# Giving out the filling products between the attention steps: the excess carried over, and a factor of 0.94 in branch A

## The chip, the cores and the metric

The kernel runs on one core of a Trainium2 chip. The metric is the device time of one execution in microseconds (us). The kernel before takes 470.46 us, the median of 3 runs (470.32 to 470.59).

## The reference

One layer of a decoder block on x of 512 tokens by 1024 channels, in float32. Two attention branches read the same normalised input and share one input projection:

```
u    = rms_norm(x, norm_pre)
proj = u @ w_in           # q_a, kv_a, g_a, z_a, qkv_b, z_b, merge
o_a  = nsa_attention(q_a, compress(...), kv_a..., gates_a)
y_a  = o_a * silu(z_a)
o_b  = moba_attention(qkv_b)
y_b  = o_b * silu(z_b)
m    = sigmoid(gate_a) * (y_a @ w_a) + sigmoid(gate_b) * (y_b @ w_b)
out  = x + rms_norm(m @ w_o, norm_post)
```

Branch A has 8 query heads of width 64 in two groups with shared keys and values. Each head has three softmaxes, over compressed blocks, over selected blocks and over a window, which are added with sigmoid gates. Branch B has 8 heads with a key and a value of their own and one softmax each. Every softmax is causal with a linear penalty for distance. At 512 tokens the selected blocks, the window and branch B's blocks cover the whole causal triangle.

## The kernel before, in words

All products have the accuracy of float32 by splitting: an operand is kept as a rounded high part and a low remainder, and one product of 128 rows is issued as three matmuls (high with high, low with high, high with low, L171 to L173, or L290 to L292 for branch B's values). A weight arrives by DMA from SyncE's queue as `raw_...`, ScalarE (ACT) writes the high part `ws_...` (L118), and VectorE (DVE) the remainder (L119).

The input projection is cut into **chunks**, each of 256 columns: za0, za1 (the gate path of branch A), vb0, vb1 (values of B), zb0, zb1 (gate path of B), qkb0 to qkb3 (queries and keys of B), ga and gb (the merge gates), and later ab and wo for the output. A chunk has two slots of eight **pieces**; a piece is a `yield 0.65`, its guess at the time, and holds three matmuls of 512 columns, twice over for six of 256 columns in vb. `stream_gen` runs through the chunks in a fixed order, and after each piece it also issues a split of the next slot's weight. When a slot is complete, the next call issues the copies out of its PSUM bank: for zb and za a tanh on ACT and a product on DVE, for qkb two or more copies on each of the two (L206 to L226), for vb eight on ACT (L305) and eight on DVE (L306).

The attention is done in 24 **units** in a software pipeline, the loop at L1047. Units 0 to 15 are branch A (`NA` = 16), even ones with the selected keys, odd ones with the window's, and units 16 to 23 are branch B. Round s of the loop issues, for the engines in this order:

- `qk_part(s, (3, 2))`: scores of query tiles 3 and 2 (L943, L944). For each, DVE adds the penalty and takes the minimum (L947), and ACT takes the exponential (L949).
- first gap: `fill(f3)`, filling pieces.
- `qk_part(s, (1, 0))`, then `norm_part(s)`: the sums' reciprocal and the normalisation of p (L955 to L961, tiles 3 and 2 on DVE, 1 and 0 on POOL). In rounds 2 and 3, the transposes of the compressed probabilities of branch A follow (L886), whose copies are `pc_...` (DVE: L892).
- second gap: `fill(f3)`.
- `pv_part(s - 2)`: the probabilities with the values (L998, L999).
- `t_part(s - 1, bank)`, three banks: transposes of p (L982, ten in a round), copied out by ACT (L983) and DVE (L984).
- third gap: `fill(f3)`.

TensorE (PE) executes this in the order in which it is written (`manual_schedule` for PE alone); ACT, DVE, POOL and the DMA issues are ordered by a scheduler at build time. PSUM has eight banks of 512 columns: three with the tag t (transposes), one o (PV), two s (scores) and two mm (the chunks). They rotate within a tag, so a matmul that begins a bank waits until the bank's former content is copied out.

What `fill` gives out is set by three lines before the change: `f3` is what is left of `total` (14 chunks at 10.4 us), shared over the remaining rounds and the three gaps of each, and

```
    def fill(us):
        while us > 0 and ("gb1" not in state["done"]):
            ...
                c = next(sg)
                us -= c
```

gives pieces until the amount is reached or exceeded. What it gives in excess is not remembered by `fill`, only in the sum `state["spent"]`, from which the next round's f3 comes.

Of the kernel before, what the change touches and what calls it, by code (L numbers as in the profile page):

```python
# [41 lines left out]
def hybrid_block(ctx, tc, x, norm_pre, w_in, pe_k, w1_k, w2_k, pe_v, w1_v, w2_v,  # L42
# [384 lines left out]
    stream = early_chunks + fill_chunks + merge_chunks + end_chunks  # L427
    pos = {c.name: i for i, c in enumerate(stream)}

    state = {"done": set(), "spent": 0.0}  # L430
    order = []
    for c in stream:
        order += [(c, 0), (c, 1)]
# [56 lines left out]
    sg = stream_gen()  # L490

    def fill(us):
        while us > 0 and ("gb1" not in state["done"]):
            try:
                c = next(sg)
                us -= c
                state["spent"] += c
            except StopIteration:
                return
# [344 lines left out]
    def cmp_scores(g):  # L844

        sp = ps("s", f"sc_{g}")
        for p in range(P):
            q = qs[f"a{p}"][:, g * 512:g * 512 + 512]
            w = slice(96 - 32 * p, 224 - 32 * p)
            mm(sp, kcs[:, g, w], q, start=(p == 0), stop=False)  # L850
            mm(sp, kcl[:, g, w], q, start=False, stop=(p == P - 1))
        both = s4.tile([128, 1024], F32, tag="s4", name=f"sc_{g}")
        bias, sc = both[:, 0:512], both[:, 512:1024]
        b = bias.rearrange("p (i h n) -> p i h n", i=4, h=4)
        for p in range(P):
            pool.tensor_scalar(b[:, :, p], distc, SL_A[4 * g + p], None, op0=ALU.mult)
        act.activation(sc, sp, AF.Copy)
        csc[g] = both

    def cmp_probs(g):  # L860

        both = csc[g]
        bias, sc = both[:, 0:512], both[:, 512:1024]
        s3 = sc.rearrange("p (a n) -> p a n", n=32)
        tp = ps("t", f"scT_{g}")
        for i in range(NT):
            pe_eng.transpose(tp[:, i * 128:(i + 1) * 128], sc[:, i * 128:(i + 1) * 128], ident)
        dve.tensor_tensor(sc, tp, bias, op=ALU.add)
        st = small.tile([128, 2, 16], F32, tag="cst", name=f"cst_{g}")
        dve.tensor_reduce(st[:, 0], s3, axis=mybir.AxisListType.X, op=ALU.min)  # L870
        dve.tensor_scalar(st[:, 0], st[:, 0], 1e20, None, op0=ALU.min)
        dve.tensor_tensor(s3, s3, st[:, 0, :, None].to_broadcast([128, 16, 32]), op=ALU.subtract)
        act.activation(sc, sc, AF.Exp, scale=-1.0)
        dve.tensor_reduce(st[:, 1], s3, axis=mybir.AxisListType.X, op=ALU.add)
        dve.tensor_scalar(st[:, 1], st[:, 1], 1e-30, None, op0=ALU.max)
        dve.reciprocal(st[:, 1], st[:, 1])
        dve.tensor_tensor(st[:, 1].rearrange("p (i h) -> p i h", i=4), st[:, 1].rearrange("p (i h) -> p i h", i=4),
                          gates[:, :, 4 * g:4 * g + 4], op=ALU.mult)
        dve.tensor_tensor(s3, s3, st[:, 1, :, None].to_broadcast([128, 16, 32]), op=ALU.mult)
        csc[g] = sc  # L880

    def cmp_transpose(g):
        sc = csc[g]
        tp = ps("t", f"tc_{g}")
        for i in range(NT):
            pe_eng.transpose(tp[:, i * 128:(i + 1) * 128], sc[:, i * 128:(i + 1) * 128], ident)  # L886

        for i in range(2):
            t = att.tile([128, T], F32R, name=f"pc_{g}_{i}")
            mine, other = slice(64 * i, 64 * i + 64), slice(64 - 64 * i, 128 - 64 * i)  # L890
            act.activation(t[mine], tp[mine], AF.Copy)
            dve.tensor_tensor(t[other], tp[mine], f(t[mine]), op=ALU.subtract)  # L892
            pcs[g, i] = t
# [27 lines left out]
    def qk_part(u, tiles):  # L921
        un = units[u]
        if NT - 1 in tiles:
            if u not in pst:
                p_start(u)
            pbig[u] = att.tile([128, 1152], F32, tag="p", bufs=2, name=f"p_{u}")
        bias = bias_of(un["bias"], un["slope"])
        h = un["half"]
        for i in tiles:
            if i == 0 and un["k"] == "kw":  # L930
                continue
            sp = ps("s", f"s_{u}_{i}")
            n = 128 * (i + 1)
            nn = max(n, 256)
            q = qs[un["q"]][:, h * 512 + i * 128:h * 512 + i * 128 + 128]
            if i == 0 and un["k"] == "ks":
                p_start(u + 1)
                hi, lo = kpair[:, h], klos[0][:, :, h, 0:128]
                todo = [(u, sp[:, 0:128]), (u + 1, sp[:, 128:256])]
            else:  # L940
                hi, lo = kst[un["k"]][:, h * 512:h * 512 + nn], klo[un["k"]][:, h, 0:nn]
                todo = [(u, sp[:, 0:n])]
            mm(sp[:, 0:nn], q, hi, start=True, stop=False)  # L943
            mm(sp[:, 0:nn], q, lo, start=False, stop=True)  # L944
            for v, src in todo:
                pp, st = p_of(v, i), pst[v]
                dve.tensor_tensor_reduce(pp, src, bias[:, 384 - 128 * i:512], 1.0, 3.0e38, ALU.add, ALU.min,  # L947
                                         st[:, 0, i:i + 1])
                act.activation(pp, pp, AF.Exp, bias=st[:, 0, i:i + 1], scale=-1.0, accum_out=st[:, 1, i:i + 1])  # L949

    def norm_part(u):
        un = units[u]
        st = pst[u]
        r = st[:, 1]
        dve.tensor_scalar(r, r, 1e-30, None, op0=ALU.max)  # L955
        dve.reciprocal(r, r)
        if un["gate"] is not None:
            dve.tensor_tensor(r, r, gates[:, :, un["gate"]], op=ALU.mult)  # L958
        for i in range(NT - 1, -1, -1):
            pp = p_of(u, i)  # L960
            (dve if i >= 2 else pool).tensor_scalar(pp, pp, st[:, 1, i:i + 1], None, op0=ALU.mult)  # L961
# [26 lines left out]
    def pv_part(u):  # L988
        un = units[u]
        first, last = un["first"], un["last"]  # L990
        if first:
            ostate["o"] = ps("o", f"o_{u}")
        o = ostate["o"]
        vn, vh = un["v"]
        v = vst[vn].rearrange("p (t h w) -> p t h w", t=4, h=2)
        for j in range(NT):
            q0 = TQ0[j]
            mm(o[:, q0 * 128:512], v[:, j, vh], pt_of(u, 0, j), start=(first and j == 0), stop=False)  # L998
            mm(o[:, q0 * 128:512], v[:, j, vh], pt_of(u, 1, j), start=False,  # L999
               stop=(last and j == 3 and un["cmp"] is None))  # L1000
        if last and un["cmp"] is not None:
            g, p = un["cmp"]
            mm(o, vcs[:, p % 2, g], pcs[g, p // 2], start=False, stop=True)
        if last:
            zt, half = un["z"]
            mine, other = slice(64 * half, 64 * half + 64), slice(64 - 64 * half, 128 - 64 * half)
            t = small.tile([128, T], F32, tag="ev", name=f"ot_{u}")
            act.activation(t[mine], o[other], AF.Copy, scale=0.5)
            dve.scalar_tensor_tensor(t[mine], o[mine], 0.5, t[mine], op0=ALU.mult, op1=ALU.add)  # L1009
            pool.tensor_tensor(zs[zt][mine], t[mine], zs[zt][mine], op=ALU.mult)  # L1010
            if half == 1 and zt >= 4:
                split_y(zt - 4)
                split_y(zt)
# [15 lines left out]
    NA = len(units)  # L1029
# [4 lines left out]
    NU = len(units)  # L1034

    state["spent"] = 0.0
    cmp_scores(0)
    fill(1.4)
    cmp_probs(0)

    def need(u):
        if u >= NA and (u - NA) % 2 == 0:
            drain_to(f"qkb{(u - NA) // 2}")

    total = sum(10.4 for c in stream[pos["za0"]:pos["gb1"] + 1])
    with tc.manual_schedule(engines={mybir.EngineType.PE}):
        for s in range(NU + 2):  # L1047
            f3 = max(0.0, total - state["spent"]) / (NU + 2 - s) / 3
            if s < NU:
                need(s)  # L1050
                qk_part(s, (3, 2))
            fill(f3)
            if s < NU:
                qk_part(s, (1, 0))
                norm_part(s)
            if s == 1:
                cmp_scores(1)
            if s in (2, 3):
                cmp_transpose(s - 2)
            if s == 1:  # L1060
                fill(f3 / 2)
                cmp_probs(1)
                fill(f3 / 2)
            else:
                fill(f3)
            if 0 <= s - 2:
                pv_part(s - 2)
            if 0 <= s - 1 < NU:
                for bank in range(3):
                    t_part(s - 1, bank)  # L1070
            fill(f3)
# [82 lines left out]
```

## Time and profile before

| | |
|---|---|
| median of 3 runs | 470.46 us (470.32 to 470.59) |
| profiled execution, its own time | 470.35 us |
| its span on the core | 468.6 us |
| granted TensorE clock, mean | 0.997 |
| PE busy | 458.2 us |
| DVE busy | 326.1 us |
| ACT busy | 253.9 us |
| POOL busy | 125.5 us |

The span is the time from the first to the last instruction on the core; 1.75 us of the execution lie around it. Times in the rows are from the span's start. PE's matmuls are pipelined, so a row's own duration is longer than its distance to the next one; the distance between starts is what a matmul costs in a row of them. In a row, "<-DVE q_b L210" in brackets says that the engine was idle for so long ahead of the instruction, and that DVE's operation of line 210 released it.

### The profile page before, as it was taken

Reading aid. Unit: us, or ns where it says so; the run is one execution under the profiler, and the core shown is the slowest. Engines: PE = TensorE matmul, PEld = TensorE weight load, DVE = VectorE, ACT = ScalarE, POOL = GpSimd, SP = SyncE. Lnnn points to the kernel's source line nnn. Section 1 sums busy time; section 2 is a strip of 40 time slices with the busy share of each in tenths; the row PEclk is TensorE's granted clock in tenths of the full one; section 3 lists DMA queues with packets and bytes.
Section 4 is the critical chain, followed back from the end, with each engine's and each line's share of the span. In section 5 each row is a group of like instructions: output and inputs, shape, how many; then the busy total and the mean of one; then the engine's idle time right before and its main releaser. Section 6 shows DMA issues by size and latency. Waiting matters only on the chain.

```text
span 468.6 us, 6999 instructions
## 1 busy us (share of the span) xinstructions
PE 458.2 (98%) x2408; PEld 389.8 (83%) x2408; DVE 326.1 (70%) x837; ACT 253.9 (54%) x684; POOL 125.5 (27%) x144
## 2 busy tenths in 40 slices
PE   8999999999999999999989999999999999999994
PEld 7888887889999888888878888888888888888884
DVE  3858767898878768878887888696674264275044
ACT  6755656666667566566667667675433333234021
POOL 6500007322432313423133454323221010020000
PEclk9999999999999999999999999999999999999998
DMA  8667125023202203032022023032135324223133
GB/s 281 187 162 199 50 50 171 8 85 91 70 21 91 72 19 90 8 84 92 19 72 90 1 90 80 12 92 80 57 94 143 109 61 134 90 90 136 45 134 136
DMA packets 45091, 42.08 MB, mean 90 GB/s; under 512 B 1624, under 2 KB 39808, under 8 KB 45056
## 3 DMA queue, kind: packets, MB, share of 16 engines
q1 hardware_dynamic: 44912, 41.12, 29.8%
q10 hardware_dynamic: 144, 0.52, 0.3%
q8 instruction: 19, 0.31, 0.3%
q14 instruction: 16, 0.13, 0.1%
HBM read 39.54 MB, written 2.10 MB: 89 GB/s over the span
## 4 chain that ended last, share of the span: by engine, by line
PE 94%; DVE 3%; POOL 1%; ACT 1%; issue 1%; POOLq 0%; DVEq 0%; ACTq 0%
PE t L982 5%; PE o L999 3%; PE o L998 3%; PE mm_gb L171 3%; PE mm_gb L173 3%; PE mm_gb L172 3%; PE s L943 3%; PE mm_qkb L171 3%; PE mm_qkb L172 3%; PE mm_qkb L173 3%; PE s L944 3%; PE mm_ga L171 3%; PE mm_ga L173 3%; PE mm_ga L172 3%; PE pa L626 2%; PE mm_vb L290 2%
## 5 line engine op out<-in xcount | busy, mean ns | idle before, releaser
L949 ACT ACTIVATE p<-p,st 128x512 f32<-128x512 f32 (+3 forms) x96 | 53.2, 555 | 45.1 <-DVE st L947 44.8
L961 POOL TENSOR_SCALAR p<-p,st 128x256 f32<-128x256 f32 (+1 forms) x48 | 43.8, 922 | 72.5 <-DVE st L958 53.3
L984 DVE TENSOR_TENSOR pt<-t,pt 128x512 fp32r<-128x512 f32 (+1 forms) x72 | 39.1, 592 | 1.9 <-ACT pt L983 1.6
L947 DVE CUSTOM_DVE_ANT_0 p<-s,bias_a 128x512 f32<-128x512 f32 (+3 forms) x64 | 29.2, 485 | 12.6 <-PE s L944 12.2
L983 ACT ACTIVATE pt<-t 128x512 fp32r<-128x512 f32 (+1 forms) x72 | 32.8, 528 | 4.8 <-PE t L982 4.2
L354 POOL TENSOR_TENSOR ga<-ga,gb 128x512 f32<-128x512 f32 x8 | 11.7, 1466 | 76.2 <-DVE gb L353 76.2
L982 PE MATMUL t<-ident,p 128*128 128x128 f32 x240 | 30.1, 273 | 0.0
L982 PEld LDWEIGHTS t<-ident,p 128*128 128x128 f32 x240 | 27.0, 140 | 0.8
L1010 POOL TENSOR_TENSOR z<-ot,z 64x512 f32<-64x512 f32 x16 | 20.7, 1295 | 24.4 <-DVE ot L1009 24.4
L171 PE MATMUL mm_qkb<-uh,ws_qkb 128*128 128x512 f32 x64 | 25.9, 405 | 1.3 <-DVE q_b L210 1.3
L119 DVE TENSOR_TENSOR ws_ab<-raw_ab,ws_ab 128x256 fp32r<-128x256 f32 x32 | 12.7, 454 | 20.0 <-ACT ws_ab L118 20.0
L171 PE MATMUL mm_ga<-uh,ws_ga 128*128 128x512 f32 x64 | 25.6, 400 | 0.0
L171 PE MATMUL mm_gb<-uh,ws_gb 128*128 128x512 f32 x64 | 25.6, 400 | 0.0
L961 DVE TENSOR_SCALAR p<-p,st 128x512 f32<-128x512 f32 (+1 forms) x48 | 24.9, 556 | 0.6
L172 PE MATMUL mm_qkb<-ul,ws_qkb 128*128 128x512 f32 x64 | 25.3, 395 | 0.0
L173 PE MATMUL mm_gb<-uh,ws_gb 128*128 128x512 f32 x64 | 25.3, 395 | 0.0
L173 PE MATMUL mm_ga<-uh,ws_ga 128*128 128x512 f32 x64 | 25.3, 395 | 0.0
L172 PE MATMUL mm_gb<-ul,ws_gb 128*128 128x512 f32 x64 | 25.3, 395 | 0.0
L172 PE MATMUL mm_ga<-ul,ws_ga 128*128 128x512 f32 x64 | 25.3, 395 | 0.0
L173 PE MATMUL mm_qkb<-uh,ws_qkb 128*128 128x512 f32 x64 | 25.3, 395 | 0.0
L901 POOL TENSOR_SCALAR bias_a<-dbase 128x512 f32<-128x512 f32 x8 | 13.2, 1650 | 32.1 <-DVE st L947 31.9
L901 POOL TENSOR_SCALAR bias_b<-dbase 128x512 f32<-128x512 f32 x8 | 12.2, 1528 | 35.5 <-DVE st L947 35.5
(312 smaller groups left out, 1386.8 us busy)
## 6 DMA issues: line engine op xcount, KB each, us to landing
raw_qkb<-in_w_in_dram SPq DMA_DIRECT2D x8, 512.0 KB, 5.1
raw_ga<-in_w_in_dram SPq DMA_DIRECT2D x4, 1024.0 KB, 5.1
raw_gb<-in_w_in_dram SPq DMA_DIRECT2D x4, 1024.0 KB, 5.2
raw_wo<-in_w_o_dram SPq DMA_DIRECT2D x4, 1024.0 KB, 5.0
raw_qa<-in_w_in_dram SPq DMA_DIRECT2D x4, 512.0 KB, 6.5
raw_za<-in_w_in_dram SPq DMA_DIRECT2D x4, 512.0 KB, 5.2
raw_vb<-in_w_in_dram SPq DMA_DIRECT2D x2, 1024.0 KB, 5.2
raw_zb<-in_w_in_dram SPq DMA_DIRECT2D x2, 1024.0 KB, 6.0
```

The lines of the kernel that those rows point to most:

```text
L171: mm(dst, v[:, 0, k], rh(n), start=(n == 0), stop=False)
L172: mm(dst, v[:, 0, k], rl(n), start=False, stop=False)
L173: mm(dst, v[:, 1, k], rh(n), start=False, stop=(n == len(kts) - 1))
L901: pool.tensor_scalar(t, dbase, slope, None, op0=ALU.mult)
L943: mm(sp[:, 0:nn], q, hi, start=True, stop=False)
L947: dve.tensor_tensor_reduce(pp, src, bias[:, 384 - 128 * i:512], 1.0, 3.0e38, ALU.add, ALU.min, st[:, 0, i:i + 1])
L949: act.activation(pp, pp, AF.Exp, bias=st[:, 0, i:i + 1], scale=-1.0, accum_out=st[:, 1, i:i + 1])
L961: (dve if i >= 2 else pool).tensor_scalar(pp, pp, st[:, 1, i:i + 1], None, op0=ALU.mult)
L982: pe_eng.transpose(tp[:, b * 128:(b + 1) * 128], p_of(u, i)[:, 128 * j:128 * j + 128], ident)
L983: act.activation(h[:, c0:c0 + n], tp[:, 0:n], AF.Copy)
L984: dve.tensor_tensor(l[:, c0:c0 + n], tp[:, 0:n], f(h[:, c0:c0 + n]), op=ALU.subtract)
L1010: pool.tensor_tensor(zs[zt][mine], t[mine], zs[zt][mine], op=ALU.mult)
```

## The change

The state gets an entry `owed`. `fill` adds its amount to it and gives pieces while it is above zero; each piece is subtracted, so that an excess stays there as a negative amount for the next call. The share f3 takes the owed amount into account and is multiplied by 0.94 in the rounds of branch A (s below 16). The whole diff:

```diff
--- before.py
+++ after.py
@@ -427,7 +427,7 @@
     stream = early_chunks + fill_chunks + merge_chunks + end_chunks
     pos = {c.name: i for i, c in enumerate(stream)}
 
-    state = {"done": set(), "spent": 0.0}
+    state = {"done": set(), "spent": 0.0, "owed": 0.0}
     order = []
     for c in stream:
         order += [(c, 0), (c, 1)]
@@ -490,10 +490,11 @@
     sg = stream_gen()
 
     def fill(us):
-        while us > 0 and ("gb1" not in state["done"]):
+        state["owed"] += us
+        while state["owed"] > 0 and "gb1" not in state["done"]:
             try:
                 c = next(sg)
-                us -= c
+                state["owed"] -= c
                 state["spent"] += c
             except StopIteration:
                 return
@@ -1045,7 +1046,8 @@
     total = sum(10.4 for c in stream[pos["za0"]:pos["gb1"] + 1])
     with tc.manual_schedule(engines={mybir.EngineType.PE}):
         for s in range(NU + 2):
-            f3 = max(0.0, total - state["spent"]) / (NU + 2 - s) / 3
+
+            f3 = max(0.0, total - state["spent"] - state["owed"]) / (NU + 2 - s) / 3 * (0.94 if s < NA else 1.0)
             if s < NU:
                 need(s)
                 qk_part(s, (3, 2))
```

One line is added above L494 and one more above L1049, so that a line of the loop's helpers, such as L947, is L948 in the changed kernel. The same instructions are issued, in another order. Pieces in a round before: nine in rounds 0 to 21 (ten in round 1), six in round 22 and the rest at the end. Now: eight in rounds 0 to 7, 9 to 11, 13 and 15, nine in rounds 8, 12, 14 and 16 to 22, and the rest at the end.

Three places show what this moves. The names: mm_ is a chunk's PSUM bank with the chunk and a running number, t_ and o_ are the banks of transposes and PV, pt0 and pt1 the transposed probabilities, st the softmax sums.

**PE, the first product of chunk zb0.** Before, in round 6:

```order
L999 MATMUL o_4_1742<-pt0_826,v_slc_126 128x256
L998 MATMUL o_4_1742<-pt0_826,v_slc_126 128x256
L999 MATMUL o_4_1742<-pt0_826,v_slc_126 128x256
L982 MATMUL t_5_0_1751<-ident_78,p0_5_1427 128x128
L982 MATMUL t_5_0_1751<-ident_78,p_5_1530 128x128 x3
L982 MATMUL t_5_1_1758<-ident_78,p_5_1530 128x128 x4
L982 MATMUL t_5_2_1765<-ident_78,p_5_1530 128x128 x2
L171 MATMUL mm_zb0_0_1778<-uh_76,ws_zb0_0_1645 128x512
```

Now, in round 7:

```order
L291 MATMUL mm_vb1_1_1578<-ws_vb1_1_1585,uh_76 128x256
L292 MATMUL mm_vb1_1_1578<-ws_vb1_1_1585,ul_77 128x256
L290 MATMUL mm_vb1_1_1578<-ws_vb1_1_1585,uh_76 128x256
L291 MATMUL mm_vb1_1_1578<-ws_vb1_1_1585,uh_76 128x256
L292 MATMUL mm_vb1_1_1578<-ws_vb1_1_1585,ul_77 128x256
L171 MATMUL mm_zb0_0_1801<-uh_76,ws_zb0_0_1709 128x512
L172 MATMUL mm_zb0_0_1801<-ul_77,ws_zb0_0_1709 128x512
L173 MATMUL mm_zb0_0_1801<-uh_76,ws_zb0_0_1709 128x512
L999 MATMUL o_4_1681<-pt1_827,v_win_127 128x512
```

Before, the products of PV and the ten transposes stand ahead of zb0's first product, now the last products of vb1, and PV follows.

**DVE, the copies out of vb1's two banks (mm_vb1_0 and mm_vb1_1).** Before, in round 6, when zb0's first product follows:

```order
L306 TENSOR_TENSOR v_b3_1692<-mm_vb1_0_1522,v_b3_1692 128x2x64
L955 TENSOR_SCALAR st_6_1655<-st_6_1655 128x4
L956 RECIPROCAL st_6_1655<-st_6_1655 128x4
L958 TENSOR_TENSOR st_6_1655<-st_6_1655,gates_103 128x4
L961 TENSOR_SCALAR p_6_1656<-p_6_1656,st_6_1655 128x512
L306 TENSOR_TENSOR v_b3_1692<-mm_vb1_0_1522,v_b3_1692 128x2x64
L961 TENSOR_SCALAR p_6_1656<-p_6_1656,st_6_1655 128x384
L306 TENSOR_TENSOR v_b2_1687<-mm_vb1_1_1523,v_b2_1687 128x2x64
```

Now, in round 7:

```order
L956 TENSOR_SCALAR st_7_1649<-st_7_1649 128x4
L306 TENSOR_TENSOR v_b3_1752<-mm_vb1_0_1577,v_b3_1752 128x2x64
L957 RECIPROCAL st_7_1649<-st_7_1649 128x4
L959 TENSOR_TENSOR st_7_1649<-st_7_1649,gates_103 128x4
L306 TENSOR_TENSOR v_b2_1747<-mm_vb1_1_1578,v_b2_1747 128x2x64
L962 TENSOR_SCALAR p_7_1726<-p_7_1726,st_7_1649 128x512
L306 TENSOR_TENSOR v_b3_1752<-mm_vb1_0_1577,v_b3_1752 128x2x64
L962 TENSOR_SCALAR p_7_1726<-p_7_1726,st_7_1649 128x384
```

Both times the last copy out of mm_vb1_0 stands between the two normalisations; now the first copy out of mm_vb1_1 is ahead of it as well, before it was behind.

**DVE, round 2, the compressed probabilities.** The two operations pc_0_0 and pc_0_1 empty the bank tc_0. Before:

```order
L119 TENSOR_TENSOR ws_vb0_1_1275<-raw_vb0_955,ws_vb0_1_1275 128x256
L892 TENSOR_TENSOR pc_0_0_1189<-tc_0_1184,pc_0_0_1189 64x512
L955 TENSOR_SCALAR st_2_1135<-st_2_1135 128x4
L119 TENSOR_TENSOR ws_vb0_1_1275<-raw_vb0_955,ws_vb0_1_1275 128x256
L956 RECIPROCAL st_2_1135<-st_2_1135 128x4
L119 TENSOR_TENSOR ws_vb0_1_1275<-raw_vb0_955,ws_vb0_1_1275 128x256
L958 TENSOR_TENSOR st_2_1135<-st_2_1135,gates_103 128x4
L892 TENSOR_TENSOR pc_0_1_1192<-tc_0_1184,pc_0_1_1192 64x512
L961 TENSOR_SCALAR p_2_1136<-p_2_1136,st_2_1135 128x512
L961 TENSOR_SCALAR p_2_1136<-p_2_1136,st_2_1135 128x384
```

Now:

```order
L119 TENSOR_TENSOR ws_vb0_0_1223<-raw_vb0_955,ws_vb0_0_1223 128x256
L956 TENSOR_SCALAR st_2_1120<-st_2_1120 128x4
L119 TENSOR_TENSOR ws_vb0_0_1223<-raw_vb0_955,ws_vb0_0_1223 128x256
L957 RECIPROCAL st_2_1120<-st_2_1120 128x4
L893 TENSOR_TENSOR pc_0_0_1172<-tc_0_1167,pc_0_0_1172 64x512
L959 TENSOR_TENSOR st_2_1120<-st_2_1120,gates_103 128x4
L119 TENSOR_TENSOR ws_vb0_0_1223<-raw_vb0_955,ws_vb0_0_1223 128x256
L962 TENSOR_SCALAR p_2_1121<-p_2_1121,st_2_1120 128x512
L962 TENSOR_SCALAR p_2_1121<-p_2_1121,st_2_1120 128x384
L893 TENSOR_TENSOR pc_0_1_1175<-tc_0_1167,pc_0_1_1175 64x512
```

Both normalisations (the last operations on p_2, of 512 and 384 columns) stood behind pc_0_1, and now stand ahead of it.

## Rows read from the trace of the kernel before

**Rows 1.** The page's first part: busy us (share) xinstructions of each engine
```profile
PE 458.2 (98%) x2408; PEld 389.8 (83%) x2408; DVE 326.1 (70%) x837; ACT 253.9 (54%) x684; POOL 125.5 (27%) x144
```

**Rows 2.** Stretches: us, PE, PEld, DVE, ACT, POOL busy (x), PEclk, DMA share, GB/s
```profile
100.70:111.10 10.40, 10.40 (x59) 9.00 (x58) 10.01 (x32) 7.05 (x20) 1.79 (x2) 1.00 0.04 5
200.00:240.00 40.00, 38.71 (x202) 32.59 (x201) 32.20 (x92) 26.53 (x74) 11.77 (x12) 1.00 0.24 71
456.00:469.00 13.00, 6.53 (x52) 6.16 (x51) 5.27 (x13) 2.22 (x8) 1.10 (x2) 0.89 0.39 142
```

**Rows 3.** Timeline, PE, round 15: start, us, engine, line, operation [idle before <-releaser]
```profile
235.61 0.40 PE L173 MATMUL mm_qkb<-uh,ws_qkb 128*128 128x512 f32 x1
237.30 0.47 PE L171 MATMUL mm_qkb<-uh,ws_qkb 128*128 128x512 f32 x1 [1.29 <-DVE q_b L210]
```

**Rows 4.** Timeline, ACT, round 15
```profile
234.53 0.59 ACT L206 ACTIVATE q_b<-mm_qkb 64x512 fp32r<-64x512 f32 x1 [0.30 <-PE s L943]
```

**Rows 5.** Timeline, DVE, round 15
```profile
236.46 0.69 DVE L210 SCALAR_TENSOR_TENSOR q_b<-mm_qkb,q_b 64x512 fp32r<-64x512 f32 x1
```

**Rows 6.** Timeline, PE, round 22
```profile
304.79 0.39 PE L173 MATMUL mm_ga<-uh,ws_ga 128*128 128x512 f32 x1
...
306.14 0.39 PE L171 MATMUL mm_ga<-uh,ws_ga 128*128 128x512 f32 x1
```

**Rows 7.** Timeline, DVE, round 22
```profile
303.30 0.69 DVE L1020 TENSOR_TENSOR ys_b<-z,ys_b 128x512 fp32r<-128x512 f32 x1 [0.83 <-ACT ys_b L1019]
...
304.57 0.68 DVE L947 CUSTOM_DVE_ANT_0 p<-s,bias_b 128x512 f32<-128x512 f32 x1
```

**Rows 8.** Timeline, PE, round 6 from its second gap
```profile
145.08 0.28 PE L290 MATMUL mm_vb<-ws_vb,uh 128*128 128x256 f32 x1
...
147.08 0.28 PE L292 MATMUL mm_vb<-ws_vb,ul 128*128 128x256 f32 x1
...
148.50 1.25 PE L982 MATMUL t<-ident,p 128*128 128x128 f32 x10
149.51 0.47 PE L171 MATMUL mm_zb<-uh,ws_zb 128*128 128x512 f32 x1
```

**Rows 9.** Timeline, DVE, round 6, after its scores
```profile
147.39 0.49 DVE L961 TENSOR_SCALAR p<-p,st 128x512 f32<-128x512 f32 x1
147.79 0.28 DVE L306 TENSOR_TENSOR v_b<-mm_vb,v_b 128x128 fp32r<-128x128 f32 x1
```

**Rows 10.** Timeline, PE, round 2
```profile
103.99 0.60 PE L886 MATMUL tc<-ident,sc 128*128 128x128 f32 x4
...
107.81 1.26 PE L982 MATMUL t<-ident,p 128*128 128x128 f32 x10
```

**Rows 11.** Timeline, DVE, round 2
```profile
103.04 0.68 DVE L879 TENSOR_TENSOR sc<-sc,cst 128x512 f32<-128x512 f32 x1
...
107.55 0.69 DVE L892 TENSOR_TENSOR pc<-tc,pc 64x512 fp32r<-64x512 f32 x1
108.28 1.08 DVE L961 TENSOR_SCALAR p<-p,st 128x512 f32<-128x512 f32 x2
```

**Rows 12.** Timeline, PE, round 0, first gap
```profile
82.43 0.40 PE L171 MATMUL mm_za<-uh,ws_za 128*128 128x512 f32 x1
...
84.54 0.28 PE L943 MATMUL s<-k_ks,q_a 128*128 128x256 f32 x1
```

**Rows 13.** Timeline, DVE, round 0
```profile
83.88 0.55 DVE L947 CUSTOM_DVE_ANT_0 p<-s,bias_a 128x384 f32<-128x384 f32 x1
```

**Rows 14.** Timeline, PE, round 6, scores and first gap
```profile
141.66 0.40 PE L943 MATMUL s<-k_ks,q_a 128*128 128x512 f32 x1
...
142.48 0.28 PE L290 MATMUL mm_vb<-ws_vb,uh 128*128 128x256 f32 x1
```

**Rows 15.** Timeline, DVE, round 6, first tile of the unit
```profile
142.59 0.68 DVE L947 CUSTOM_DVE_ANT_0 p<-s,bias_a 128x512 f32<-128x512 f32 x1
```

**Rows 16.** Timeline, DVE, qkb3's k copies
```profile
238.04 0.68 DVE L223 TENSOR_TENSOR klos<-mm_qkb,k_b 64x512 fp32r<-64x512 f32 x1
```

## The prediction

> **What bounds the kernel now.** I read the busy times first. TensorE (PE) is busy for 458.2 of the 468.6 us of the span, VectorE (DVE) for 326.1, ScalarE (ACT) for 253.9 [rows 1]. The reader should see that this leaves PE 10.4 us without work in all. The table by stretches says where: PE is busy in all of 10.40 us in round 2 of the attention loop, in 38.71 of 40 us between 200 and 240 us, and in only 6.53 of the last 13 us, at a granted clock of 1.00, 1.00 and 0.89 [rows 2]. The change does not touch the last 13 us nor the first products. So the loop is a solid row of matmuls, and a change of order alone can win only the few gaps in it. The start times of neighbouring matmuls show them: 512 columns follow each other in 0.234 us (from 82.43 to 84.54 us, nine of them [rows 12]), 256 columns in 0.118 (seventeen in 2.00 us [rows 8]). Only two places in the loop lie more than 0.4 us above this.
>
> Gap one is in round 15. The first product of chunk qkb3 starts 1.69 us after the matmul ahead of it [rows 3]; less the usual 0.23 that is 1.46 us. It waits for its PSUM bank: ACT copies qkb2's query half out of it only at 234.53 [rows 4], and DVE takes the second half of the remainder at 236.46 for 0.69 us [rows 5]. The matmuls into that bank were done in round 14; the copies stood behind unit 15's exponentials on ACT. Gap two is in round 22: five matmuls (one of 512, four of 256 columns) take 1.35 us from 304.79 to 306.14 [rows 6], where 0.23 + 4 x 0.118 = 0.70 is usual, so 0.65 us is lost. Unit 22's first score tile leaves its bank on DVE at 304.57, behind a split of a branch product at 303.30 that had itself waited for ACT [rows 7].
>
> **The change part by part.** No instruction is added or removed; filling pieces (0.70 us of PE each) move. Before, every call rounds up to whole pieces, so nine stand in nearly every round until they run short in round 22 (six). Now the excess is remembered and the share is cut to 0.94 in branch A: eight in most of rounds 0 to 15 and nine in rounds 16 to 22. After round 15 there are 131 pieces handed out instead of 145, and the 14 missing ones fill rounds 22 to 24. Their weight splits (ACT and DVE) and DMA loads move with them, later in number of rounds; DMA is busy for 0.24 of 200 to 240 us and 0.04 of round 2 [rows 2], so I cost the loads at nothing. If that cover failed, a chunk's first product would wait for a load, and I see no load near its due time.
>
> *Gain, round 15.* qkb2's query half is now finished in round 16's first gap, its copies stand behind two of unit 16's exponentials, and the bank is next wanted in round 17, some 9 us of PE work later. The 1.46 us go. *Gain, round 22.* Its first gap has three pieces instead of two and no branch split ahead of the score: 0.65 us go; at least 0.4, if that bank stays a little late. Together 2.1 us (1.85 to 2.1); I take 2.05.
>
> *New wait, round 7 (second gap).* Chunk zb0 now follows the last product of vb1 directly. In round 6 before, PV and the transposes stood between: vb1's last product started at 147.08, zb0's first at 149.51 [rows 8]. With X the end of the scores (145.08), DVE finished the last copy of vb1's bank 0 at 147.79 + 0.28 = X + 2.99 [rows 9], 1.4 us before it was needed. Now the bank is wanted after two pieces, at X + 12 x 0.118 = X + 1.41, and on DVE the last copy of bank 0 stands behind bank 1's first copy, and, as before, the 512-column normalisation. From below: bank 1's last product ends at X + 1.57, then an ACT copy (taken as 0.28, like its DVE remainder), the remainder (0.28), the normalisation (0.40 from its start to the next) and the last copy (0.28) give X + 2.8, a wait of 1.4 [rows 9]. From above: the old X + 2.99 plus the copy put ahead (0.28) is X + 3.3, a wait of 1.9. I take 1.7, since DVE has little slack.
>
> *New wait, round 2 (transposes).* The third transpose bank is the one that the compressed scores' transposes used. These started at 103.99, and the transposes at 107.81, at 0.1 us each, so the third bank was wanted after eight, at 108.6, which is 4.6 after 103.99 [rows 10]. DVE freed it with its second pass at 107.55 + 0.69 = 108.24, 4.25 after [rows 11]. Only 0.35 us was to spare. Now both normalisations (1.08 us) and a 0.68 us addition that used to run earlier, at 103.04, stand ahead of that pass [rows 11], while a 0.68 us operation on za moves behind it: 4.25 + 1.08 = 5.3 after, a wait of 0.7, and without credit for the za operation, and with the wait for the reciprocal, up to 6.4, a wait of 1.8. I take 1.5, near the upper end, since DVE has 10.01 us of work in a round of 10.40 [rows 2] and does not catch up.
>
> *New wait, round 0.* With two pieces in the first gap instead of three, the last score tile wants its bank after 6 x 0.234 + 2 x 0.118, at 84.07 by the old times [rows 12]. DVE frees it at 83.88 + 0.55 = 84.43 [rows 13]. 0.4 us (0.2 to 0.6).
>
> *New wait, round 6 (first gap).* vb1's second bank is wanted one piece after the scores: 0.82 (from 141.66 to 142.48) + 0.70 = 1.52 us after the scores start [rows 14]. The last copy out of it now stands behind the unit's first tile, which DVE started 0.93 us after the scores, for 0.68 [rows 15]; with 0.28 for the copy it is free at 1.8 to 1.9. 0.3 us (0 to 0.6).
>
> *Rounds 2 (scores) and 19.* A few DVE operations that fell elsewhere now stand ahead of a unit's first tile: four weight splits on ACT in round 2, the k copies of qkb3 in round 19 (0.68 for one of 512 columns [rows 16]). One such operation late at worst, nothing at best: 0.2 each (0 to 0.6).
>
> Sum of the new waits: 0.4 + 0.2 + 1.5 + 0.3 + 1.7 + 0.2 = 4.3 us (2.3 to 6.1). Net: 4.3 - 2.05 = +2.25. The profiled execution took 470.35 us, so 472.6; the median is 0.11 above it, so **472.7 us**. The unknown ends give 470.6 (2.3 with a gain of 2.1) to 474.7 (6.1 with 1.85).
>
> **A rule that speaks against the change.** The row first: after the 1.29 us wait in round 15 the granted clock of 200 to 240 us still reads 1.00 [rows 2, 3]. In a sentence by itself: the Trainium skill, "TensorE: Matmul & The Clock Gate", section "A second HAM failure mode: psum-queue depth-cycling", says that a TensorE which idles briefly between groups while it cycles through PSUM banks swings between its clock levels and loses throughput beyond the idling. By that rule the new bank waits would cost more than their length; by the row they cost their length, and that is what I add.
>
> **The rivals.** *The new waits are hidden* (the other side, faster). The mechanism is the copy out of a bank in time, and round 7 decides: if DVE finishes bank 0 within 1.41 us of the scores, and the third transpose bank comes within 4.6 us of the compressed transposes, 0.5 us of the rest remains: 470.46 - 2.05 + 0.5 = 468.9. Break-even is at 2.05 us of new waits. For it: these engines are ordered by a scheduler, and delays met early give DVE time to catch up later. Against it: DVE's order in both rounds puts the freeing pass behind work that cannot start sooner. *The balance*: the new waits stay near their low ends, 1.2 to 2.9 in sum: 469.6 to 471.4, no change that can be told. *DVE becomes the bound of rounds 1 to 3*: eight pieces make a round 0.70 us shorter, 10.40 - 0.70 = 9.70, under DVE's 10.01 [rows 2], and the lag is paid in each of these rounds: 8 x 0.3 = 2.4 us more if eight rounds are as full, 475.1. For it: the row. Against it: later rounds leave DVE more slack, and splits move out with the pieces. *The clock falls* after a 2 us wait: one round of about 10 us at half rate, 483. Against it: the row of round 15. *The change doesn't do what it says*: the order shows that the pieces move, so I give this nothing.
>
> **How the numbers follow.** A measurement of this kernel can tell 0.2% (0.94 us) from no change. Forecast as it stands, slower, 471.4 to 474.7: 0.50. DVE as the bound: 0.14. Clock: 0.04. Balance, within 0.2%: 0.20. Hidden, faster: 0.12. So slower is 0.68. The range leaves out the clock and the ends of the two neighbours, about 0.2 in all: 469.6 to 475.2; the forecast's own is 471.4 to 474.7.
>
> **What would show it.** Right: no wait of qkb3's first product on DVE in the list of waits, and none over 0.3 us in round 22; instead a stop of 1.4 to 1.9 us ahead of zb0's first product put down to DVE's copies of vb, one of 0.7 to 1.8 inside a set of ten transposes in round 2 put down to the compressed pass, and one near 0.4 in round 0. PE's busy time stays near 458 and the span grows. Wrong: no stop ahead of zb0, or a granted clock under 1.00 inside the loop, or waits spread over many rounds with DVE full.

## The result, and the profile after

The changed kernel takes 473.11 us (median of 4 runs, 472.98 to 473.47), the kernel before 470.39 us (4 runs, 470.32 to 470.59): a ratio of 1.0058, 95% interval 1.0046 to 1.0070. It is slower by 2.7 us. The profiled execution took 473.22 us with a span of 471.4.

The busy times of the changed kernel (us, share of the span, instructions), to compare with [rows 1]:

```profile
PE 460.7 (98%) x2408; PEld 390.8 (83%) x2408; DVE 326.3 (69%) x837; ACT 254.5 (54%) x684; POOL 126.3 (27%) x144
```

The same 2408 matmuls are busy for 2.5 us more. What that means is said at the end; the stops are better read from the starts of matmuls. The list of waits (engine, operation and line <- what released it: us in total, times, longest) has lost the wait of qkb3's first product, and has new ones:

```profile
PE mm_zb L171 <- DVE v_b L306: 1.4, 1, 1.4
...
PE s L944 <- DVE st L948: 0.5, 2, 0.3
...
PE t L983 <- DVE pc L893: 0.5, 1, 0.5
```

In stretches (us, then PE, PEld, DVE, ACT and POOL busy, granted clock, DMA share, GB/s), the gap of [rows 2] between 200 and 240 us is closed. Most of the loop's idle time now lies between 70 and 160 us (the loop starts at 81.7, round 7 ends near 159). The granted clock is 1.00 in both kernels. First the kernel before, then the changed one:

```profile
70.00:160.00 90.00, 89.80 (x561) 80.00 (x560) 75.25 (x229) 59.16 (x174) 33.65 (x39) 1.00 0.24 70
```

```profile
70.00:160.00 90.00, 87.51 (x546) 77.48 (x546) 75.00 (x228) 58.34 (x170) 35.96 (x40) 1.00 0.24 71
200.00:240.00 40.00, 40.00 (x213) 34.29 (x213) 32.48 (x97) 25.49 (x72) 13.79 (x13) 1.00 0.19 53
```

**The largest new stop** is in round 7, ahead of zb0's first product. PE first, then DVE:

```profile
151.27 0.28 PE L945 MATMUL s<-klos,q_a 128*128 128x256 f32 x1
...
152.69 0.28 PE L292 MATMUL mm_vb<-ws_vb,ul 128*128 128x256 f32 x1
154.37 0.47 PE L171 MATMUL mm_zb<-uh,ws_zb 128*128 128x512 f32 x1 [1.40 <-DVE v_b L306]
```

```profile
153.35 0.28 DVE L306 TENSOR_TENSOR v_b<-mm_vb,v_b 128x128 fp32r<-128x128 f32 x1
153.55 0.48 DVE L962 TENSOR_SCALAR p<-p,st 128x512 f32<-128x512 f32 x1
153.94 0.28 DVE L306 TENSOR_TENSOR v_b<-mm_vb,v_b 128x128 fp32r<-128x128 f32 x1
```

PE has done with vb1 at 152.69 and starts zb0 1.68 us later, where 0.12 is usual. DVE makes the last copy of bank 0 at 153.94, behind bank 1's first copy (153.35) and the normalisation of 512 columns (153.55). It ends at 154.22, and zb0 follows 0.15 later. With X the end of the scores, 151.39 (one distance of 0.12 behind the last score matmul at 151.27), the bank was free at X + 2.8.

**Round 2**, inside the ten transposes, PE and DVE:

```profile
105.95 1.04 PE L983 MATMUL t<-ident,p 128*128 128x128 f32 x8
107.48 0.41 PE L983 MATMUL t<-ident,p 128*128 128x128 f32 x2 [0.49 <-DVE pc L893]
```

```profile
104.31 0.68 DVE L893 TENSOR_TENSOR pc<-tc,pc 64x512 fp32r<-64x512 f32 x1
...
105.44 1.17 DVE L962 TENSOR_SCALAR p<-p,st 128x512 f32<-128x512 f32 x2
106.64 0.69 DVE L893 TENSOR_TENSOR pc<-tc,pc 64x512 fp32r<-64x512 f32 x1
107.36 0.69 DVE L237 SCALAR_TENSOR_TENSOR z<-sg,mm_za 128x512 f32<-128x512 f32 x1
```

Eight transposes start in a row, 0.109 us apart. The ninth should start at 105.95 + 8 x 0.109 = 106.82 and starts at 107.48, 0.66 us late, when DVE has ended its second compressed pass (106.64 + 0.69 = 107.33). Both normalisations (105.44) stand ahead of that pass; the operation on za (107.36) now stands behind it.

**Round 0 and round 6.** The last score tile of round 0 (84.68) follows 0.53 us behind its neighbour instead of 0.12. In round 6 the first product into vb1's second bank (140.32) comes 0.42 after the one ahead of it:

```profile
84.15 0.28 PE L945 MATMUL s<-klos,q_a 128*128 128x256 f32 x1
84.68 0.38 PE L944 MATMUL s<-kpair,q_a 128*128 128x256 f32 x1 [0.25 <-DVE st L948]
```

```profile
139.90 0.28 PE L292 MATMUL mm_vb<-ws_vb,ul 128*128 128x256 f32 x1
140.32 0.36 PE L290 MATMUL mm_vb<-ws_vb,uh 128*128 128x256 f32 x1
```

**Round 4**, which the prediction does not name, DVE and PE:

```profile
120.47 0.67 DVE L237 SCALAR_TENSOR_TENSOR z<-sg,mm_za 128x512 f32<-128x512 f32 x1
```

```profile
121.19 0.39 PE L290 MATMUL mm_vb<-ws_vb,uh 128*128 128x256 f32 x1
```

The operation on za1 (120.47 + 0.67 = 121.14) empties the bank that becomes vb0's second. The first product into it starts at 121.19, 0.26 us behind the matmul ahead of it, and the next one follows 0.23 later, where 0.12 is usual both times. Together 0.25 us are lost.

**Round 19**, which I had put at 0.2 us. PE, and DVE just before:

```profile
268.02 0.40 PE L173 MATMUL mm_ga<-uh,ws_ga 128*128 128x512 f32 x1
268.71 0.39 PE L944 MATMUL s<-k_b,q_b 128*128 128x256 f32 x1 [0.29 <-DVE st L948]
...
269.52 0.40 PE L171 MATMUL mm_ga<-uh,ws_ga 128*128 128x512 f32 x1
```

```profile
265.53 0.42 DVE L225 CAST k_b<-k_b 64x512 fp32r<-64x512 f32 x1
...
266.79 0.69 DVE L224 TENSOR_TENSOR klos<-mm_qkb,k_b 64x512 fp32r<-64x512 f32 x1
267.50 0.42 DVE L226 CAST k_b<-k_b 64x512 fp32r<-64x512 f32 x1
267.95 0.69 DVE L948 CUSTOM_DVE_ANT_0 p<-s,bias_b 128x512 f32<-128x512 f32 x1
```

All four operations on qkb3's keys (265.53 to 267.92) stand ahead of unit 19's first tile (267.95). The second of its two score matmuls starts at 265.58, the next matmul at 265.81. From 268.02 to 269.52 PE needs 1.50 us for five matmuls that usually take 0.70: 0.80 us are lost.

**Round 22**, whose gap I had taken for closed, PE and DVE:

```profile
298.66 0.40 PE L173 MATMUL mm_gb<-uh,ws_gb 128*128 128x512 f32 x1
299.04 0.39 PE L944 MATMUL s<-k_b,q_b 128*128 128x256 f32 x1
...
299.86 0.40 PE L171 MATMUL mm_gb<-uh,ws_gb 128*128 128x512 f32 x1
```

```profile
297.36 0.69 DVE L1021 TENSOR_TENSOR ys_b<-z,ys_b 128x512 fp32r<-128x512 f32 x1 [0.82 <-ACT ys_b L1020]
...
298.30 0.68 DVE L948 CUSTOM_DVE_ANT_0 p<-s,bias_b 128x512 f32<-128x512 f32 x1
```

1.20 us for the same five matmuls: 0.50 us are still lost, against 0.65 in [rows 6]. The split of the branch product (297.36) is still ahead of the score tile (298.30), as in [rows 7].

The gap that did close is the one ahead of qkb3: its first product starts at 246.74, 0.24 us behind the matmul ahead of it. DVE's last copy out of its bank now ends at 241.03 + 0.69 = 241.72, 5.0 us earlier:

```profile
241.03 0.69 DVE L210 SCALAR_TENSOR_TENSOR q_b<-mm_qkb,q_b 64x512 fp32r<-64x512 f32 x1
```

```profile
246.74 0.40 PE L171 MATMUL mm_qkb<-uh,ws_qkb 128*128 128x512 f32 x1
```

### The profile page after: what moved, and what is told of

It reads as the page before. It is cut to its first block, busy times and chain, and to the rows that moved or that the text cites. A ratio compares the mean times of both kernels' runs of the same rounds, so it can differ in the third digit from the quotient of the medians.

```text
span 471.4 us, 6998 instructions
## 1 busy us (share of the span) xinstructions
PE 460.7 (98%) x2408; PEld 390.8 (83%) x2408; DVE 326.3 (69%) x837; ACT 254.5 (54%) x684; POOL 126.3 (27%) x144
## 4 chain that ended last, share of the span: by engine, by line
PE 89%; DVE 7%; ACT 2%; issue 1%; POOL 0%; POOLq 0%; DVEq 0%; ACTq 0%
PE t L983 5%; PE mm_gb L171 3%; PE mm_qkb L171 3%; PE mm_gb L172 3%; PE mm_gb L173 3%; PE mm_qkb L172 3%; PE mm_qkb L173 3%; PE o L999 3%; PE o L1000 3%; PE mm_ga L173 3%; PE mm_ga L171 3%; PE mm_ga L172 3%; PE s L944 3%; PE pa L627 3%; PE s L945 3%; PE mm_zb L171 2%
## 5 line engine op out<-in xcount | busy, mean ns | idle before, releaser
L962 POOL TENSOR_SCALAR p<-p,st 128x256 f32<-128x256 f32 (+1 forms) x48 | 45.4, 955 | 62.8 <-DVE st L959 31.4
L948 DVE CUSTOM_DVE_ANT_0 p<-s,bias_a 128x512 f32<-128x512 f32 (+3 forms) x64 | 29.2, 487 | 13.8 <-PE s L945 13.8
```

## The experiments

Each kernel was run five to nine times, in turn with the kernel before. That one took 470.43 us (9 runs, 470.33 to 470.76) beside "Order on DVE alone" and "All named stops", and 470.34 us (18 runs, 470.01 to 470.98) beside the others. "Pieces 3, 2, 3" means the filling pieces in the three gaps of a round. In the kernels with moved pieces, `fill` takes the number of pieces from a table, which is the kernel's own but for the entries named.

**The factor without the carry** needs no run. It changes nothing: in round 0 a gap's share is 145.6 / 78 = 1.87 us, and 0.94 of it 1.75; both round up to three pieces of 0.65, and the later calls round up alike. The built program has the same instructions in the same order on PE, DVE and ACT as the kernel before.

**The carry without the factor.**

```diff
-            f3 = ... / (NU + 2 - s) / 3 * (0.94 if s < NA else 1.0)
+            f3 = ... / (NU + 2 - s) / 3
```

> The change with the carried excess but the factor 0.94 taken out. Theory (single stops of TensorE at banks that are emptied late, which depend on where a chunk's boundary falls): other boundaries, so other stops. None ahead of zb0's first product and none ahead of qkb3's; 0.5 us in round 0 (two pieces in the first gap again); 1.4 to 2.0 us among round 2's transposes, since its second gap has two pieces instead of three and the bank is wanted 0.7 us sooner; 0.5 us in round 22. In sum about 471.1 us (470.4 to 471.8). Rival (DVE is the bound in rounds of eight pieces, so the loss goes with the number of such rounds): it loses about half of what the change loses, 471.7, spread over rounds 0 to 15 with no stop over 0.5 us.

Measured: 473.39 us, ratio 1.0065 (1.0052 to 1.0077). Both were wrong on the time: the theory by 2.3 us. The stops that it named came, 0.53 us in round 0, 1.76 in round 2 and 0.58 in round 22, but also two that it did not name, 1.2 us in round 12 and 0.9 in round 20. Round 2, then round 12, each PE and DVE:

```profile
106.41 1.04 PE L983 MATMUL t<-ident,p 128*128 128x128 f32 x8
109.05 0.41 PE L983 MATMUL t<-ident,p 128*128 128x128 f32 x2 [1.60 <-DVE pc L893]
```

```profile
105.36 1.04 DVE L962 TENSOR_SCALAR p<-p,st 128x512 f32<-128x512 f32 x2
...
107.15 0.69 DVE L237 SCALAR_TENSOR_TENSOR z<-sg,mm_za 128x512 f32<-128x512 f32 x1
...
108.21 0.69 DVE L893 TENSOR_TENSOR pc<-tc,pc 64x512 fp32r<-64x512 f32 x1
```

```profile
191.71 0.39 PE L173 MATMUL mm_zb<-uh,ws_zb 128*128 128x512 f32 x1
193.08 0.38 PE L944 MATMUL s<-k_kw,q_a 128*128 128x256 f32 x1 [0.98 <-DVE st L948]
```

```profile
189.85 0.42 DVE L225 CAST k_b<-k_b 64x512 fp32r<-64x512 f32 x1 [0.37 <-ACT k_b L221]
...
191.87 0.42 DVE L226 CAST k_b<-k_b 64x512 fp32r<-64x512 f32 x1
192.32 0.69 DVE L948 CUSTOM_DVE_ANT_0 p<-s,bias_a 128x512 f32<-128x512 f32 x1
```

In round 2 the normalisations and the operation on za both stand ahead of the second compressed pass (108.21). In round 12 the chunk qkb0 ends just ahead of the scores, and its four key operations stand ahead of unit 12's first tile, the pattern of round 19 in the changed kernel. The rival falls by the trace: the loss is in five single stops of over 0.5 us each, not spread. It falls by the number of rounds too: this kernel has eight pieces in 8 of the 16 rounds of branch A, the changed kernel in 13, and it loses 3.05 us against 2.72. So it is not the factor that costs; with the full share other boundaries meet, and cost as much.

**One piece moved out of the changed kernel's largest stop.** Round 7: pieces 3, 2, 3 instead of 3, 3, 2.

```diff
-    ..., 3, 3, 2, ...
+    ..., 3, 2, 3, ...
```

> The changed kernel with one filling piece, zb0's first, moved from the second to the third gap of round 7, behind PV and the transposes. Theory: the stop of 1.57 us ahead of it is gone and nothing takes its place: 473.1 - 1.6 = 471.5 us (471.3 to 471.9). Rival (DVE is behind in these rounds, the stop is only where it shows): the lag shows up at the next wait for DVE, and 472.5 to 473.1 remain.

Measured: 471.50 us (9 runs, 471.30 to 472.18), as the theory said. zb0's first product now follows the transposes at their usual distance, with no wait named; the other stops of the changed kernel stand as they were:

```profile
154.75 1.25 PE L982 MATMUL t<-ident,p 128*128 128x128 f32 x10
155.75 0.48 PE L171 MATMUL mm_zb<-uh,ws_zb 128*128 128x512 f32 x1
```

**The same stop put into the kernel before.** Round 6: pieces 3, 4, 2 instead of 3, 3, 3.

```diff
-    ..., 3, 3, 3, ...
+    ..., 3, 4, 2, ...
```

> The kernel before with one filling piece, zb0's first, moved from the third to the second gap of round 6, directly behind vb1's last product. Theory: DVE frees the bank 2.99 us after the scores, and it is now wanted after three pieces, at 2.12: a stop of 0.9 to 1.0 us that the kernel before does not have, 471.35 us (471.2 to 471.6), at nine pieces a round as before. Rival (only rounds of eight pieces are short of time): no stop over 0.3 us, 470.4.

Measured: 471.44 us (9 runs, 471.39 to 472.12); before, on the same chip, 470.34 (18 runs). It is 1.1 us slower, as the theory said. The stop is there, 1.14 - 0.12 = 1.02 us, at nine pieces a round:

```profile
147.76 0.28 PE L292 MATMUL mm_vb<-ws_vb,ul 128*128 128x256 f32 x1
148.90 0.47 PE L171 MATMUL mm_zb<-uh,ws_zb 128*128 128x512 f32 x1 [0.86 <-DVE v_b L306]
```

**Order on DVE alone.** In the changed kernel the compressed transposes are written ahead of the normalisation:

```diff
                 qk_part(s, (1, 0))
+                if s in (2, 3):
+                    cmp_transpose(s - 2)
                 norm_part(s)
...
-            if s in (2, 3):
-                cmp_transpose(s - 2)
```

> The changed kernel with the compressed probabilities' transposes written ahead of the normalisation of the same round, so that DVE's pass that empties the bank stands ahead of the two normalisations in round 2, with the operation on za (0.69 us) now ahead of that pass. TensorE's order is unchanged. Theory: the bank is free 1.17 - 0.69 = 0.5 us sooner, so of the 0.66 us some 0.15 are left: 472.6 us (472.3 to 473.0), all other stops as in the changed kernel. Rival (the transposes wait for something else there, p of the unit before or the ACT copy): 0.66 us stay, 473.1.

Measured: 472.50 us (5 runs, 472.49 to 472.65), 0.6 below the changed kernel. The stop among the transposes shrank from 0.66 to 0.30 us (0.15 was expected) with PE's order unchanged, so it is DVE's pass that they wait for; the row of all ten is 1.58 us long, where 1.25 is usual. The operation on za and the pass now come first:

```profile
105.76 1.58 PE L983 MATMUL t<-ident,p 128*128 128x128 f32 x10
```

```profile
105.37 0.69 DVE L237 SCALAR_TENSOR_TENSOR z<-sg,mm_za 128x512 f32<-128x512 f32 x1
106.09 0.69 DVE L893 TENSOR_TENSOR pc<-tc,pc 64x512 fp32r<-64x512 f32 x1
106.82 0.81 DVE L962 TENSOR_SCALAR p<-p,st 128x512 f32<-128x512 f32 x2
```

The rest of the 0.6 us is the small stop of 0.25 us in round 4, which this kernel does not have either.

**All named stops of the changed kernel taken out**, by moving single pieces, with eight pieces still in most rounds of branch A:

```diff
-    2, 3, 3   (round 0)
+    3, 2, 3
-    2, 3, 3   (round 2)
+    2, 4, 2
...
-    3, 3, 3   (round 22)
+    4, 2, 3
```

> The changed kernel with the same number of pieces in each of rounds 8 to 17 and some 8 in rounds 0 to 7, but single pieces moved at six places: round 0 gives 3, 2, 3 pieces in its gaps instead of 2, 3, 3; round 2 gives 2, 4, 2; rounds 5 and 6 give 3, 2, 2 and 3, 4, 2; round 7 3, 2, 3; rounds 18 and 19 3, 3, 2 and 4, 3, 3; round 22 4, 2, 3. Theory (single stops): the stops of 0.52 (round 0), 0.66 (round 2), 0.30 (round 6), 1.57 (round 7), 0.81 (round 19) and 0.50 us (round 22) go, 4.36 in sum: 473.1 - 4.4 = 468.7 us (468.5 to 469.4). Rival (eight pieces a round leave DVE short of time): the stops turn up elsewhere in rounds 0 to 15, over 471 us.

Measured: 468.96 us (5 runs, 468.91 to 468.98), ratio 0.9967 (0.9955 to 0.9980). The six stops are gone; 0.37 us in round 4, at the same bank as in the changed kernel, are the only stop of over 0.25 left. The six were taken out together, so the shares of rounds 0, 6, 19 and 22 rest on the distances between starts and not on runs of their own. PE between 70 and 160 us is busy for 89.69 of 90 us, with DVE at 77.22, more than in the changed kernel:

```profile
70.00:160.00 90.00, 89.69 (x561) 79.85 (x559) 77.22 (x236) 59.62 (x175) 36.06 (x40) 1.00 0.24 71
```

**The kernel before with its two gaps closed.**

```diff
-    3, 3, 3   (round 15)
+    3, 2, 4
-    2, 2, 2   (round 22)
+    3, 2, 2
```

> The kernel before with its two gaps closed by hand: in round 15 qkb3's first piece moved from the second to the third gap, in round 22 three pieces in the first gap instead of two, the rest as before. Theory: 1.46 us and 0.65 us go and no new stop comes: 468.3 us (468.2 to 468.8). Rival (a stop removed turns up at the next wait): 469.5 to 470.4.

Measured: 468.78 us (6 runs, 468.60 to 469.40), ratio 0.9968 (0.9956 to 0.9979). The DVE copy that qkb3 waits for starts at 236.36, 0.1 us before the start in [rows 5], and ends at 237.05; the product now comes 1.2 us behind that, after PV and the transposes:

```profile
237.26 1.25 PE L982 MATMUL t<-ident,p 128*128 128x128 f32 x10
238.26 0.48 PE L171 MATMUL mm_qkb<-uh,ws_qkb 128*128 128x512 f32 x1
```

Both gaps are gone (2.1 us) and two small ones of 0.25 us stand in the scores near 244 and 265 us (before, 0.16 at the second). That should win 1.8 us; by the medians it is 1.6, in the theory's range at its upper end, and where the other 0.2 went was not looked into. This and the kernel above are the fastest, by 1.5 us against the kernel before.

## Why the prediction was right, and where it was not

472.7 us were forecast and 473.11 measured, for the reason given: TensorE runs back to back, so a change of order can only remove or make stops, and the new boundaries of the chunks make more than they remove. Stops below are distances between starts less the usual distance, summed over the place.

| place | forecast, us | measured, us |
|---|---|---|
| round 15, qkb3 (gain) | 1.46 | 1.46 |
| round 22, scores (gain) | 0.65 | 0.15 |
| round 7, zb0 behind vb1 | 1.7 (1.4 to 1.9) | 1.57 |
| round 2, transposes | 1.5 (0.7 to 1.8) | 0.66 |
| round 0, score tile | 0.4 (0.2 to 0.6) | 0.52 |
| round 6, vb1's second bank | 0.3 (0 to 0.6) | 0.30 |
| round 2, scores | 0.2 (0 to 0.6) | 0.19 |
| round 19, scores | 0.2 (0 to 0.6) | 0.80 |
| round 4, vb0's second bank | not named | 0.25 |

The new stops sum to 4.29 us (forecast 4.3) and the gains to 1.61 (forecast 2.05), net 2.68. The last matmul starts at 465.11 instead of 462.25 us, 2.86 later; 0.19 of that lies ahead of the loop, where nothing was changed. The loop alone is 2.67 longer, so the sum closes.

- **Gain, round 15**: right, by the list of waits, by qkb3's first product and by the copy that ends 5.0 us ahead of it.
- **Gain, round 22**: the step failed that said there was "no branch split ahead of the score". The rows show one, L1021 at 297.36. I had looked at which weight splits moved away, not at the branch product's own.
- **Round 7**: right, mechanism and size. The bank was free at X + 2.8, the lower bound's own figure, since unit 7 has no tile 0 and its sums were ready early (DVE takes them up at 152.69, X + 1.3). The kernels that move one piece out of it and one into the kernel before show that this order alone makes the stop.
- **Round 2, transposes**: right place, too large. I leaned to the upper end because DVE had 10.01 us of work in a round of 10.40. The lower end held, the one that credits the operation on za moved behind the pass: free 5.2 us after the compressed transposes. How full an engine is over a round was the wrong row to choose by; the order of its operations had the answer. That the pass is the cause is shown by writing it earlier.
- **Round 19**: the sum took one late operation; four stood there, with 0.42 + 0.68 + 0.69 + 0.42 us.
- **Round 4**: not in the sum. The prediction followed the reuse of vb1's and zb0's banks, not that of vb0's second bank behind za1.
- **Two slips that no term hangs on**: the 14 pieces that move out of branch A fill rounds 22 to 25, not 22 to 24, and DVE's "addition" at 103.04 is a multiplication (L879) of the length given.
- **The rival that DVE becomes the bound** fell: with eight pieces still in most of those rounds and the stops moved away the kernel takes 468.96 us.
- **The rival that the clock falls** fell: the granted clock reads 1.00 between 70 and 160 us with 2.5 us of idle PE in it. The rule of the Trainium skill's page "TensorE: Matmul & The Clock Gate", section "A second HAM failure mode: psum-queue depth-cycling", would make the clock swing at such bank stops and so cost more than their length; no run here shows that.
- **PE's busy time** did not stay near 458 as I had said; see below.

That the new stops sum to 4.29 us against 4.3 was luck: the transposes of round 2 came 0.84 short, and rounds 19 and 4 brought 0.60 and 0.25 more. The sign did not hang on it: without that 0.85 the new stops still exceed the gains.

## What to carry to other kernels

Where one engine is busy throughout, a new order is priced by its stops: for every buffer that is reused, compare when it is wanted with the place of the operation that empties it in the other engine's order, not with that engine's load. Here a smoother distribution lost 2.7 us and the same one with a few pieces moved won 1.5, so check such a rule by the boundaries it makes (a chunk's end directly ahead of the next chunk's start, or of a score tile), and give the first product of a new chunk a place behind other work.

## What the runs showed of the hardware that I had not expected

Of a stop only that part appears as idle time which exceeds the row of the matmul ahead: in round 7 1.68 us between starts less a row of 0.28 gives the 1.40 shown. The stops of round 4 (0.26 us between starts) and of round 22 show none. Round 19 lost 0.80 us by its starts, and its row names an idle time of 0.29; the same matmuls in the same number count 2.5 us more busy time in the changed kernel, 0.75 of it in the first 26 us, which the change does not touch (24.04 against 23.29 us busy).

The matmul behind the one that waited also follows late: 0.22 us behind a 256-column matmul in rounds 0, 19 and 22 where 0.12 is usual, so several short waits in a row cost more than the sum of their idle times. It is not the stop alone that does this: behind ten transposes, with no stop, the first 512-column product is followed after 0.32 us (97.07 to 97.39 in the changed kernel) where 0.23 is usual. The cause stays open.
